# W_out's sums spread over all pairs with two sets of buffers; loads pinned behind operand loads; operands split three steps ahead

## The chip, the cores and the metric

The kernel runs on one core of one Trainium2 chip. The metric is the time of one execution on the device in microseconds, the median of several runs. The core has five engines that run their own instruction streams in order: TensorE (PE, matmuls), VectorE (DVE), ScalarE (ACT), GpSimd (POOL) and SyncE (SP, which here only issues DMAs). The program is written with tiles; a scheduler orders each engine's instructions by their place in the program and by when they are ready, and inserts the waits.

## The reference

One layer of an encoder on a sequence of 1024 tokens of width 1024, in float32. All three sub-layers stand between norms:

```
x = x + 1/2 * post1(SwiGLU_1(pre1(x)))      # feed-forward, D_FF = 2816
x = x + post_mix(token_mixing(pre_mix(x)))   # retention and neighbourhood attention
x = x + 1/2 * post2(SwiGLU_2(pre2(x)))      # feed-forward, D_FF = 2816

def _swiglu(x, w_in, w_out):
    g, u = jnp.split(x @ w_in, 2, axis=-1)
    return (jax.nn.silu(g) * u) @ w_out

def _rms_norm(x, gain):
    y = x * lax.rsqrt(jnp.mean(x * x, axis=-1, keepdims=True) + RMS_EPS)
    return y * gain
```

The change touches the two feed-forward sub-layers only.

## The kernel before, in words

Every float32 operand is split into a high and a low part (`Core.split`, lines 60 and 61: a cast on ACT, then a subtraction on DVE), and each product is three matmuls (`mm3`, lines 87 to 89: high x high, low x high, high x low). A matmul here has 128 x 128 weights and 512 columns. The large products use the Winograd form of Strassen's scheme: seven half-sized products and a number of sums in place of eight products.

A feed-forward has two stages.

`ffn_in` computes silu(x Wg) * (x Wu), transposed, in 22 *pairs* (a gate block and an up block of 128 features, index i). In one pair `Pairs.run` does seven products of twelve matmuls (P1, P6, P2, P7, P5, P4, P3 in this order); DVE makes the weight-side sums in place in the raw weights (`wraw`), splits them (`wh`, `wl`, eight buffers each), and adds the results up. `done(j)` is called as a quarter of the result is ready, in the order 0, 3, 1, 2; with j = 1 and 2 it multiplies gate and up into the tile `gt` (line 416). After every second pair `LeftFactors` makes four sums of two `gt` tiles on POOL (tile `cmb`, line 440) and stores seven blocks to DRAM (`g0a`, `g0s`; in the second feed-forward `g1a`, `g1s`) with DMAs that POOL issues (line 67). These are the left operands of the next stage.

In passing, `ffn_in` also prepares the weight-side sums of `W_out` for the next stage: `OutSums` takes eleven sets of four 128 x 512 blocks of `W_out`, loads them (line 521, SP), makes four subtractions on DVE (line 524) and stores the four results to DRAM (POOL, tensor `t`). Before the change it is a generator that does one step (four loads, or one subtraction with its store) at each call of `done`, four in a pair, from pair 6 on in the first feed-forward and from pair 4 on in the second. Its tiles are `lead` in the pool `early` in the first (six buffers, shared with what the lead products save), `tw` in the second (four buffers). Nothing fixes where in its engine's order a step comes; the scheduler may move it forward.

`ffn_out` computes the down-projection in seven products (a11, s1, s2, s3, a22, a12, s4) of eleven *steps* each, 77 in all. A step takes one left block (`Blocks`: load `graw` on SP, split into `gh`, `gl`) and one weight block (`wraw`, split into `wh`, `wl`), and does twelve matmuls, three into each of four banks. `operand(n)` prepares step n; before the change, steps n and n + 1 are prepared ahead of the matmuls of step n. There are four buffers for `gh` and `gl`: three in the pool `gl10` and one in `gl11` in the first feed-forward, two in `gl20` and two in `gl21` in the second. After the eleventh step of a product, its handler (p1, p5, p6, p7, p4, p2, p3) takes the four banks out on ACT or DVE; `more` in p7 queues two further sums and a square for each of four token tiles, which are taken up one per step from product a22 on. `Epilogue` holds the norm: gains (loaded in step 11), squares on ACT (line 481) with a product with the gain (line 482, POOL unless told otherwise), and the residual. The rows of x for it come by `xload` in the steps 30 to 36 and 57 to 63 of the program.

Memory: pools lie in stacks from the left and the right. In the first feed-forward the left stack holds, from the same base, first `norm1`, then `fin1` (`c0` and `c1` with two 2 KB buffers each, `gt` with three of 4 KB: 20 KB per partition), then the pools of `ffn_out`: 20 KB (`mid0`), then `gl10` with 18 KB. In the second, `cmb2` (8 KB) and `tw2` (8 KB) lie below `fin2` (20 KB), and the pools of `ffn_out` begin with 36 KB (`out2`), then `gl21` with 12 KB; `gl20` is on the right. A tile of a new pool may be written as soon as the old tiles under it are released.

Of the kernel before, what the change touches and what calls it, by code (L numbers as in the profile page):

```python
# [10 lines left out]
F32 = mybir.dt.float32  # L11
F32R = mybir.dt.float32r
AF = mybir.ActivationFunctionType
ALU = mybir.AluOpType
# [4 lines left out]
P = 128  # L19
# [5 lines left out]
FT = DFF // P  # L25
# [12 lines left out]
class Core:  # L38
# [131 lines left out]
class Filler:  # L170
# [13 lines left out]
    def __call__(self, n):  # L184
        for _ in range(n):
            if not self.step():
                return
# [216 lines left out]
def ffn_in(c, pairs, pool, put, sums):  # L404

    nc = c.nc
    for i in range(FT):
        gate = [pool.tile([P, 512], F32, tag=f"c{j}", name=f"c{j}", bufs=2) for j in range(2)]
        gt = pool.tile([P, S], F32, tag="gt", name="gt", bufs=3)
        up = gt[:, :512], gt[:, 512:]  # L410

        def done(j):
            if j < 2:
                nc.scalar.activation(gate[j], gate[j], AF.Silu)  # L414
            if j in (1, 2):
                nc.vector.tensor_tensor(up[j % 2], gate[j % 2], up[j % 2], ALU.mult)
            sums(i)
        pairs.run(i, (*gate, *up).__getitem__, done)
        put(i, gt)

# [24 lines left out]
class Blocks:  # L445
# [6 lines left out]
    def __call__(self, src):  # L452
        p = self.pools[self.n % len(self.pools)]
        self.n += 1
        r = p.tile([P, 512], F32, tag="graw", name="graw", bufs=self.raws[p is not self.pools[0]])
        self.c.nc.sync.dma_start(r, src)
        a = [p.tile([P, 512], F32R, tag=g, name=g, bufs=self.pools.count(p)) for g in ("gh", "gl")]
        self.c.split(*a, r)
        return a
# [47 lines left out]
class OutSums:  # L507


    def __init__(self, c, tile, src, dst, first):  # L510
        self.first, self.left = first, self.steps(c, tile, src, dst)

    @staticmethod
    def steps(c, tile, src, dst):

        tt = c.nc.vector.tensor_tensor
        for k in range(FT // 2):
            ks = slice(k * 512, (k + 1) * 512)
            b11, b12, b21, b22 = b = [tile() for _ in range(4)]
            for q in range(4):  # L520
                c.nc.sync.dma_start(b[q], src[q][:, ks])
            yield
            for n, o, x, y in ((0, b11, b12, b11), (2, b12, b22, b12), (1, b22, b22, b11), (3, b21, b21, b22)):
                tt(o, x, y, ALU.subtract)
                c.store(dst[n][:, ks], o)
                yield

    def __call__(self, i):
        if i >= self.first:
            next(self.left, None)  # L530


def ffn_out(c, q, blocks, junk, xtile, w_out, t_out, gl, ep, side={}):


    nc = c.nc
    NK = FT // 2
    tt, add = nc.vector.tensor_tensor, nc.gpsimd.tensor_tensor
    later, rest, flips, xs = [], [], [], {}

    def xload(t):

        xs[t] = xtile(t)
        nc.sync.dma_start(xs[t], ep.resid(t))


    def p1(u, b):
        nc.scalar.copy(q[0][:, u], b)

    def p6(u, b):  # L550
        tt(q[1][:, u], b, q[0][:, u], ALU.add)

    def p5(u, b):
        nc.scalar.copy(q[2][:, u], b)

    def p7(u, b):
        tt(q[3][:, u], b, q[1][:, u], ALU.add)

        def more():
            add(q[1][:, u], q[1][:, u], q[2][:, u], ALU.add)  # L560
            add(q[2][:, u], q[3][:, u], q[2][:, u], ALU.add)
            ep.square(u, 1, q[2][:, u], junk[u])
        later.extend((more, None))

    def p4(u, b):
        tt(q[3][:, u], b, q[3][:, u], ALU.add)
        ep.square(u, 0, q[3][:, u], b)
        later.extend(stages(u, (q[3][:, u], q[2][:, u])))

    def stages(t, halves):  # L570
        g = ep.steps(t, xs[t], halves)

        f = []
        return [lambda: next(g), lambda: next(g)] + [
            lambda: f.append(next(g)), lambda: f[0](*(("ps", 6) if i < 6 else ("pt", 2)))] * (ep.pre is not None)

    def p2(u, b):
        tt(q[0][:, u], b, q[0][:, u], ALU.add)
        ep.square(4 + u, 0, q[0][:, u], b)

    def p3(u, b):
        e = tt(q[1][:, u], b, q[1][:, u], ALU.add)
        out = q[1][:, u] if ep.pre is not None else q[3][:, u]
        ep.square(4 + u, 1, q[1][:, u], b if ep.pre is not None else junk[2 + u % 2], out, nc.vector if u == 3 else nc.gpsimd)
        g = ep.steps(4 + u, xs[4 + u], (q[0][:, u], out))
# [12 lines left out]
    steps = [(i, k) for i in range(len(products)) for k in range(NK)]  # L598
    xloads = {n: j for j, n in enumerate((30, 32, 34, 36, 57, 59, 61, 63))}
    operands, raws, banks, last = {}, {}, {}, []  # L600

    def wraw(n):

        if n not in raws:
            raw = c.wpool.tile([P, D], F32, tag="wraw", name="wraw", bufs=3)
            (i, k), two = steps[n], n + 1 < len(steps) and steps[n][1] < NK - 1
            nc.sync.dma_start(raw[:, :512 + 512 * two], products[i][1][:, k * 512:(k + 1 + two) * 512])
            raws[n] = raw[:, :512]
            if n + 1 < len(steps):
                if not two:  # L610
                    nc.sync.dma_start(raw[:, 512:], products[i + 1][1][:, :512])
                raws[n + 1] = raw[:, 512:]
        return raws.pop(n)

    def operand(n):
        if n < len(steps) and n not in operands:
            i, k = steps[n]
            operands[n] = blocks(gl[products[i][0]][:, k * 512:(k + 1) * 512]), c.piece(wraw(n))

    def one(u, k, a, b):  # L620
        c.mm3(banks[u], [p[:, u * P:(u + 1) * P] for p in a], b, k == 0, k == NK - 1)

    for n, (i, k) in enumerate(steps):
        for m in range(2):
            operand(n + m)
        if n == NK:
            ep.gains()
        if n in side:
            side[n]()
        if n in xloads:  # L630
            xload(xloads[n])
        if later and i > 3:
            f = later.pop(0)
            if f:
                f()
        if k == 0:
            banks = {u: c.bank() if i % 2 == 0 or u < 2 else c.bank("pt", 2) for u in range(4)}
        ab = operands.pop(n)
        if i == len(products) - 1 and k >= NK - 4:
            last.append((k, *ab))  # L640
        else:
            for u in range(4):
                one(u, k, *ab)
        if k == NK - 1:
            operand(n + 2)
            for u in range(4):
                for e in last:
                    one(u, *e)
                products[i][2](u, banks[u])
    assert not later  # L650
    return flips
# [354 lines left out]
def trunk_layer(ctx: ExitStack, tc, x, g1a, w1i, w1o, g1b, gma, wmt, wnv, wrv, logits, dtab, rope, bias,  # L1006
                wro, wno, wmo, gmb, g2a, w2i, w2o, g2b, out):
    nc = tc.nc
# [36 lines left out]
    with tc.tile_pool(name="norm1", bufs=1, reuse_waits="tile") as ep:  # L1045
# [7 lines left out]
                f()  # L1053
        fin = Pairs(c, wx, [(w1i[i], w1i[FT + i]) for i in LeftFactors.order], 3, 3)
        fin.lead(lambda: early.tile([P, 512], F32, tag="lead", name="lead", bufs=6), on_pool=(3, 4, 5, 0))
    with tc.tile_pool(name="fin1", bufs=1, reuse_waits="tile") as fp:
        ffn_in(c, fin, fp, LeftFactors(c, early, gl[0]),
               OutSums(c, lambda: early.tile([P, 512], F32, tag="lead", name="lead", bufs=6), w1o, t1o, 6))
    right.close()

    x0pool = pool(right, "x0", "right")
# [4 lines left out]
    ep = pool(ep_stack, "ep1", "right")  # L1066
# [244 lines left out]
    tw = pool(left, "tw2")  # L1311
    with tc.tile_pool(name="fin2", bufs=1, reuse_waits="tile") as fp:
        ffn_in(c, fin, fp, LeftFactors(c, cmb, gl[1]),
               OutSums(c, lambda: tw.tile([P, 512], F32, tag="tw", name="tw", bufs=4), w2o, t2o, 4))
    left.close()
    a_stack.close()
    g_stack.close()
# [89 lines left out]
```

## Time and profile before

| | us |
|---|---|
| median of 3 runs (lowest, highest) | 2358.86 (2357.84, 2363.87) |
| the profiled execution | 2363.65 |
| its span, first to last instruction | 2361.9 |
| PE busy | 2240.7 |
| DVE busy | 1704.5 |
| ACT busy | 1001.7 |
| POOL busy | 626.7 |

The first `ffn_in` runs from about 60 us to 486 us of the span, its `ffn_out` to about 740; the token mixing follows; the second `ffn_in` runs from about 1707 to 2137 us, and its `ffn_out` to the end. A row of stretches gives the busy time of each engine and, behind x, the number of its instructions in that stretch. A row of waits names the waiting engine with its line, what released it, the sum, the number and the longest. A row of the timeline gives start and duration in us and, in brackets, how long the engine was idle before and what ended it. A row of a tile gives the shortest, median and longest duration in ns, and the first and last start in us. PE instructions overlap, so PE counts as busy at a low clock too; the number of matmuls in a stretch tells more.

### The profile page before, as it was taken

To read this page: it belongs to the slowest core of one execution; us is meant where nothing else is said; L and a number is where in the kernel's file an instruction comes from. 1 tells how busy PE (TensorE), PEld (TensorE's weight loads), DVE (VectorE), ACT (ScalarE), POOL (GpSimd) and SP (SyncE) were. 2 spreads that over 40 slices of the span, in tenths; PEclk is the share of its full clock that TensorE was granted. 3 is DMA by queue.
4 is the path that set the end of the run, shared out by engine and by line. 5 is a ranking of instruction groups with operands and counts; after the bars stand their busy time and mean duration, and the time that the engine had idled before them with its cause. 6 is when DMAs were issued, how large, how long until landed. Compare 5 with 4: busy or idle time off the path is not lost.

```text
span 2361.9 us, 30397 instructions
## 1 busy us (share of the span) xinstructions
PE 2240.7 (95%) x10288; PEld 1846.2 (78%) x10288; DVE 1704.5 (72%) x2921; ACT 1001.7 (42%) x2102; POOL 626.7 (27%) x713
## 2 busy tenths in 40 slices
PE   6998899989998999999999999999799999999998
PEld 5776688868777787787888888887577778888876
DVE  7887686645588758879985678547898787665566
ACT  6332232334455323248885675226533232234443
POOL 5243331310224123411101222101533323221042
PEclk9999999989999999999999999999899999999999
DMA  4357632376564443247755467856466543337655
GB/s 143 132 191 240 231 130 95 122 254 190 175 200 139 164 161 112 103 160 241 232 178 170 156 221 236 292 208 207 155 218 211 199 148 123 104 122 272 192 161 172
DMA packets 163677, 422.64 MB, mean 179 GB/s; under 512 B 19713, under 2 KB 47489, under 8 KB 163457
## 3 DMA queue, kind: packets, MB, share of 16 engines
q1 hardware_dynamic: 130080, 310.04, 41.2%
q0 software_dynamic: 33440, 110.65, 11.9%
q8 instruction: 81, 1.33, 0.2%
q14 instruction: 76, 0.61, 0.1%
HBM read 301.60 MB, written 123.21 MB: 180 GB/s over the span
## 4 chain that ended last, share of the span: by engine, by line
PE 63%; DVE 13%; issue 8%; POOL 8%; DMA 6%; ACT 2%; SPq 0%; POOLq 0%; DVEq 0%; ACTq 0%
PE ps L89 19%; PE ps L87 19%; PE ps L88 19%; DVE wl L61 2%; POOL cmb L440 2%; PE pt L87 1%; PE pt L88 1%; PE pt L89 1%; POOL rstd L97 1%; PE ps L721 1%; PE pt L740 1%; DMA t<-tw 1%; POOL t L67 1%; DMA graw<-g0a 1%; DMA t<-lead 1%
## 5 line engine op out<-in xcount | busy, mean ns | idle before, releaser
L61 DVE TENSOR_TENSOR wl<-wraw,wh 128x512 fp32r<-128x512 f32 x662 | 491.9, 764 | 81.3 <-ACT wh L60 80.2
L60 ACT CAST wh<-wraw 128x512 fp32r<-128x512 f32 x670 | 391.1, 617 | 244.5 <-PE ps L88 84.3
L61 DVE TENSOR_TENSOR gl<-graw,gh 128x512 fp32r<-128x512 f32 (+2 forms) x178 | 130.9, 736 | 188.8 <-ACT gh L60 188.6
L87 PE MATMUL ps<-wh,gh 128*128 128x512 f32 x612 | 241.9, 397 | 15.7 <-ACT gh L60 14.6
L89 PE MATMUL ps<-wh,gl 128*128 128x512 f32 x612 | 241.3, 397 | 4.2 <-DVE gl L61 3.9
L88 PE MATMUL ps<-wl,gh 128*128 128x512 f32 x612 | 241.2, 395 | 2.0 <-DVE wl L61 2.0
L60 ACT CAST gh<-graw 128x512 fp32r<-128x512 f32 (+2 forms) x178 | 107.0, 601 | 234.5 <-PE ps L88 100.2
L414 ACT ACTIVATE c<-c 128x512 f32<-128x512 f32 x88 | 55.6, 632 | 296.9 <-DVE c L384 199.1
L87 PEld LDWEIGHTS ps<-wh,gh 128*128 128x128 f32 x612 | 116.7, 191 | 43.1 <-ACT gh L60 17.3
L89 PEld LDWEIGHTS ps<-wh,gl 128*128 128x128 f32 x612 | 116.6, 191 | 33.2 <-DVE gl L61 8.9
L88 PEld LDWEIGHTS ps<-wl,gh 128*128 128x128 f32 x612 | 116.8, 191 | 26.8 <-DVE wl L61 3.1
L60 ACT CAST wh<-t 128x512 fp32r<-128x512 f32 x58 | 36.1, 622 | 220.2 <-DVE t L378 218.8
L89 PE MATMUL ps<-s2h,wl 128*128 128x512 f32 x232 | 97.5, 420 | 21.4 <-DVE wl L61 21.4
L89 PE MATMUL ps<-a12h,wl 128*128 128x512 f32 x280 | 110.6, 395 | 3.7 <-DVE wl L61 3.7
L87 PE MATMUL ps<-a11h,wh 128*128 128x512 f32 x280 | 111.9, 400 | 1.4 <-ACT wh L60 0.7
L87 PE MATMUL ps<-a12h,wh 128*128 128x512 f32 x280 | 111.5, 398 | 0.0
L89 PE MATMUL ps<-a11h,wl 128*128 128x512 f32 x280 | 110.5, 395 | 0.7 <-DVE wl L61 0.7
L88 PE MATMUL ps<-a11l,wh 128*128 128x512 f32 x280 | 110.8, 396 | 0.0
L88 PE MATMUL ps<-a12l,wh 128*128 128x512 f32 x280 | 110.0, 393 | 0.0
L87 PE MATMUL ps<-a22h,wh 128*128 128x512 f32 x280 | 109.8, 392 | 0.0
L89 PE MATMUL ps<-a22h,wl 128*128 128x512 f32 x280 | 109.1, 390 | 0.0
L88 PE MATMUL ps<-a22l,wh 128*128 128x512 f32 x280 | 109.0, 389 | 0.0
(356 smaller groups left out, 5969.8 us busy)
## 6 DMA issues: line engine op xcount, KB each, us to landing
wraw<-in_dram SPq DMA_DIRECT2D x243, 512.0 KB, 4.4
wraw<-t SPq DMA_DIRECT2D x40, 512.0 KB, 3.7
lead<-in_dram SPq DMA_DIRECT2D x44, 256.0 KB, 4.0
g0s<-cmb POOLq DMA_DIRECT2D x44, 256.0 KB, 2.5
t<-lead POOLq DMA_DIRECT2D x44, 256.0 KB, 3.5
graw<-g0s SPq DMA_DIRECT2D x44, 256.0 KB, 2.8
tw<-in_dram SPq DMA_DIRECT2D x44, 256.0 KB, 3.4
t<-tw POOLq DMA_DIRECT2D x44, 256.0 KB, 3.7
```

The costliest lines, as they stand in the source:

```text
L60: nc.scalar.copy(h, src)
L61: (eng or nc.vector).tensor_tensor(l, src, hf, ALU.subtract)
L67: self.nc.gpsimd.dma_start(dst, src)
L87: mm(ps, a[0], b[0], start=start, stop=False)
L88: mm(ps, a[0], b[1], start=False, stop=False)
L89: mm(ps, a[1], b[0], start=False, stop=stop)
L97: self.nc.gpsimd.tensor_tensor(r[:, :n], ms, self.mhalf[:, :n], ALU.pow)
L414: nc.scalar.activation(gate[j], gate[j], AF.Silu)
L440: eng.tensor_tensor(s[o], a, b, op)
L721: nc.tensor.matmul(bv, q[:, rg * P:(rg + 1) * P], k, start=n == 0, stop=n == 1)
L740: nc.tensor.transpose(pt[:, j * P:(j + 1) * P], s[:, i % 2, (i // 2) * P:(i // 2 + 1) * P], c.ident)
```

## The change

`OutSums` is rewritten. Set 0 is loaded in pair 0, set k in pair 2k - 1; set 0 is subtracted in pair 1, two subtractions each at `done(1)` and `done(2)`; set k in pairs 2k and 2k + 1, one at each of these. The call is made inside `issue_after(e.ins)`, which puts what the call makes on the engine of `e` (DVE) behind `e`, the product that has just written `gt`; it is an order in that engine's queue, not a wait. The loads (SP) and stores (POOL) are on other engines. There are eight buffers (two sets) in both feed-forwards; in the first they are a pool of their own, `tw1`, opened below `fin1`.

In `ffn_out` the loads of x and of the gains are put behind the last operand load on SP, the operands of steps n, n + 1 and n + 2 are prepared ahead of the matmuls of step n (and n + 3 ahead of a product's handler), and the sums and the gain product of `more` go from POOL to DVE.

```diff
@@ ffn_in
             if j in (1, 2):
-                nc.vector.tensor_tensor(up[j % 2], gate[j % 2], up[j % 2], ALU.mult)
-            sums(i)
+                e = nc.vector.tensor_tensor(up[j % 2], gate[j % 2], up[j % 2], ALU.mult)
+                with c.tc.issue_after(e.ins):
+                    sums(i, j)
@@ Blocks
-        self.c.nc.sync.dma_start(r, src)
+        self.load = self.c.nc.sync.dma_start(r, src)
@@ OutSums
-        for k in range(FT // 2):
...
-            for n, o, x, y in ((0, b11, b12, b11), (2, b12, b22, b12), (1, b22, b22, b11), (3, b21, b21, b22)):
-                tt(o, x, y, ALU.subtract)
-                c.store(dst[n][:, ks], o)
-                yield
-    def __call__(self, i):
-        if i >= self.first:
-            next(self.left, None)
+    def load(self, k):
+        self.b[k] = [self.tile() for _ in range(4)]
+        for t, src in zip(self.b[k], self.src):
+            self.c.nc.sync.dma_start(t, src[:, k * 512:(k + 1) * 512])
+    def sub(self, k, n):
+        b11, b12, b21, b22 = self.b[k]
+        o, x, y = ((b11, b12, b11), (b22, b22, b11), (b12, b22, b12), (b21, b21, b22))[n]
+        self.c.nc.vector.tensor_tensor(o, x, y, ALU.subtract)
+        self.c.store(self.dst[n][:, k * 512:(k + 1) * 512], o)
+    def __call__(self, i, j):
+        if j == 1 and (i == 0 or i % 2 == 1 and i < FT - 2):
+            self.load((i + 1) // 2)
+        for n in ((0, 2), (1, 3))[j - 1] if i == 1 else ():
+            self.sub(0, n)
+        if i > 1:
+            self.sub(i // 2, (0, 2, 1, 3)[i % 2 * 2 + j - 1])
@@ ffn_out
         xs[t] = xtile(t)
-        nc.sync.dma_start(xs[t], ep.resid(t))
+        with c.tc.issue_after(blocks.load.ins):
+            nc.sync.dma_start(xs[t], ep.resid(t))
...
-            add(q[1][:, u], q[1][:, u], q[2][:, u], ALU.add)
-            add(q[2][:, u], q[3][:, u], q[2][:, u], ALU.add)
-            ep.square(u, 1, q[2][:, u], junk[u])
+            tt(q[1][:, u], q[1][:, u], q[2][:, u], ALU.add)
+            tt(q[2][:, u], q[3][:, u], q[2][:, u], ALU.add)
+            ep.square(u, 1, q[2][:, u], junk[u], eng=nc.vector)
...
-        for m in range(2):
+        for m in range(3):
             operand(n + m)
         if n == NK:
-            ep.gains()
+            with c.tc.issue_after(blocks.load.ins):
+                ep.gains()
...
-            operand(n + 2)
+            operand(n + 3)
@@ trunk_layer
+    with (tc.tile_pool(name="tw1", bufs=1, reuse_waits="tile") as tw,
+          tc.tile_pool(name="fin1", bufs=1, reuse_waits="tile") as fp):
-               OutSums(c, lambda: early.tile([P, 512], F32, tag="lead", name="lead", bufs=6), w1o, t1o, 6))
+               OutSums(c, lambda: tw.tile([P, 512], F32, tag="tw", name="tw", bufs=8), w1o, t1o))
...
-               OutSums(c, lambda: tw.tile([P, 512], F32, tag="tw", name="tw", bufs=4), w2o, t2o, 4))
+               OutSums(c, lambda: tw.tile([P, 512], F32, tag="tw", name="tw", bufs=8), w2o, t2o))
```

More of the change, by code (lines that the diff above doesn't have):

```diff
@@ L507, with __init__ @@
 class OutSums:
[L510 to L516, printed above, removed]
-        for k in range(FT // 2):
[L518 to L521, printed above, removed]
-            yield
-            for n, o, x, y in ((0, b11, b12, b11), (2, b12, b22, b12), (1, b22, b22, b11), (3, b21, b21, b22)):
-                tt(o, x, y, ALU.subtract)
-                c.store(dst[n][:, ks], o)
-                yield
-    def __call__(self, i):
-        if i >= self.first:
-            next(self.left, None)
+    def __init__(self, c, tile, src, dst):
+        self.c, self.tile, self.src, self.dst, self.b = c, tile, src, dst, {}
+    def load(self, k):
[14 more added lines that the diff above has]
+            self.sub(i // 2, (0, 2, 1, 3)[i % 2 * 2 + j - 1])
 def ffn_out(c, q, blocks, junk, xtile, w_out, t_out, gl, ep, side={}):
@@ L537, in ffn_out @@
     NK = FT // 2
-    tt, add = nc.vector.tensor_tensor, nc.gpsimd.tensor_tensor
+    tt = nc.vector.tensor_tensor
     later, rest, flips, xs = [], [], [], {}
@@ L1055, in trunk_layer @@
         fin.lead(lambda: early.tile([P, 512], F32, tag="lead", name="lead", bufs=6), on_pool=(3, 4, 5, 0))
-    with tc.tile_pool(name="fin1", bufs=1, reuse_waits="tile") as fp:
+    with (tc.tile_pool(name="tw1", bufs=1, reuse_waits="tile") as tw,
+          tc.tile_pool(name="fin1", bufs=1, reuse_waits="tile") as fp):
         ffn_in(c, fin, fp, LeftFactors(c, early, gl[0]),
-               OutSums(c, lambda: early.tile([P, 512], F32, tag="lead", name="lead", bufs=6), w1o, t1o, 6))
+               OutSums(c, lambda: tw.tile([P, 512], F32, tag="tw", name="tw", bufs=8), w1o, t1o))
     right.close()
```

## The prediction

> **What bounds the kernel now.** I read the page's busy times first, then stretches of the span, then who waited for whom inside the bad stretches, then the timeline of single gaps.
>
> ```profile
> span 2361.9 us, 30397 instructions
> ```
> ```profile
> PE 2240.7 (95%) x10288; PEld 1846.2 (78%) x10288; DVE 1704.5 (72%) x2921; ACT 1001.7 (42%) x2102; POOL 626.7 (27%) x713
> ```
>
> TensorE is the bound, and its 95% hides how much it misses: at a low clock its instructions last longer and still count as busy. So I count matmuls in stretches that lie where the change acts (columns: start:end, length, then busy us and count for PE, weight loads, DVE, ACT, POOL, then granted clock, DMA share, GB/s).
>
> ```profile
> 130.00:310.00 180.00, 161.13 (x666) 129.73 (x665) 139.03 (x211) 45.79 (x81) 74.84 (x91) 0.94 0.64 223
> 310.00:480.00 170.00, 170.00 (x752) 140.76 (x751) 120.09 (x183) 53.70 (x94) 42.95 (x51) 1.00 0.33 116
> 480.00:511.00 31.00, 20.89 (x81) 16.66 (x80) 13.63 (x17) 7.45 (x13) 8.71 (x10) 0.78 0.74 257
> 511.00:620.00 109.00, 109.00 (x482) 90.26 (x481) 55.53 (x87) 49.41 (x88) 1.29 (x1) 1.00 0.66 209
> 620.00:640.00 20.00, 16.75 (x66) 12.63 (x65) 12.62 (x12) 8.58 (x19) 16.04 (x11) 0.93 0.26 70
> 1712.00:1732.00 20.00, 17.44 (x71) 14.03 (x70) 19.35 (x27) 8.78 (x14) 7.09 (x7) 0.91 0.45 158
> 1732.00:1930.00 198.00, 184.69 (x781) 148.46 (x780) 161.36 (x239) 54.24 (x98) 73.55 (x95) 0.97 0.61 207
> 1930.00:2130.00 200.00, 200.00 (x884) 165.62 (x883) 138.48 (x214) 62.70 (x110) 48.57 (x56) 1.00 0.32 113
> 2130.00:2250.00 120.00, 120.00 (x531) 99.34 (x531) 64.31 (x96) 53.18 (x95) 8.71 (x10) 1.00 0.71 236
> 2258.00:2278.00 20.00, 16.79 (x66) 12.63 (x65) 12.60 (x12) 8.58 (x19) 16.01 (x11) 0.94 0.26 73
> ```
>
> The row from 310 shows TensorE undisturbed: 752 matmuls in 170 us, 0.226 us each. That is the second half of the first up-projection (`ffn_in`), after the old `OutSums` had ended; 1930 to 2130 is the same place in the second. Against 0.226 us the other rows are short:
> - A, 130 to 310, `ffn_in` with the sums of `W_out`: 796 fit, 666 ran, 130 x 0.226 = 29.4 us lost.
> - B, 1732 to 1930, the same in the second: 876 against 781, 21.5 us.
> - C, 480 to 511, where the first `ffn_out` begins: 137 against 81, 12.7 us.
> - D, 620 to 640 and 2258 to 2278, after product `s3` of each `ffn_out`: 88.5 against 66, 5.1 us each.
> - E, 1712 to 1732, the start of the second `ffn_in`: 88.5 against 71, 4.0 us.
> - 2130 to 2250, where the second `ffn_out` begins: 531 of 531, nothing lost.
>
> In all 77.8 us are on the table. Now the causes of A and B: VectorE's waits in 130 to 310, SyncE's queue there, and VectorE's in 1730 to 1930.
>
> ```profile
> DVE lead L524 <- DMA lead<-in_dram: 35.1, 7, 7.9
> ```
> ```profile
> SPq L521 <- DMA t<-lead: 74.0, 30, 11.2
> ```
> ```profile
> DVE tw L524 <- DMA tw<-in_dram: 21.4, 9, 6.2
> DVE gl L61 <- ACT gh L60: 9.2, 2, 6.0
> ```
>
> VectorE works in order, and it stands for 35.1 and 21.4 us behind a subtraction whose block hasn't landed. The block is late because its load waits on SyncE for the store of the previous block from the same buffer: six buffers for sets of four in the first stage, four in the second. One gap, on SP, DVE and PE:
>
> ```profile
> 207.29 23.19 SPq L521 DMA_DIRECT2D lead<-in_dram  x6
> ```
> ```profile
> 222.83 0.69 DVE L524 TENSOR_TENSOR lead<-lead 128x512 f32<-128x512 f32 x1 [7.90 <-DMA lead<-in_dram]
> ```
> ```profile
> 225.38 0.79 PE L89 MATMUL ps<-s2h,wl 128*128 128x512 f32 x1 [6.56 <-DVE wl L61]
> 225.97 0.63 PE L87 MATMUL ps<-s2h,wh 128*128 128x512 f32 x1
> 226.39 0.63 PE L88 MATMUL ps<-s2l,wh 128*128 128x512 f32 x1
> ```
>
> SP spends 23 us over six loads, DVE waits 7.90 us, the split of P6's weights is late, PE stands 6.56 us and then starts matmuls every 0.42 us instead of 0.226: each gap is paid a second time in clock.
>
> **The change, part by part.**
>
> *Sums of W_out.* As many instructions as before: 44 loads, 44 subtractions, 44 stores per stage. Now set k is loaded in pair 2k-1 and subtracted in pairs 2k and 2k+1, two per pair, over all 22 pairs. A set of buffers comes round again only after its stores have had a whole pair (19 us) to land, and a load has a pair to land; the longest waits shown are 7.9 and 11.2 us. So the waits of A and B should go. What it costs where there were no sums (310 to 480): two subtractions a pair on DVE.
>
> ```profile
> L524 DVE TENSOR_TENSOR lead<-lead x44: 674/692/1798, 120.4 to 303.2; 128x512 f32<-128x512 f32 x44
> ```
>
> 2 x 0.692 = 1.4 us a pair; DVE was busy 120.09 of 170 us there, so idle 49.9 us, or 5.6 us in each of nine 19 us pairs. The pin puts a subtraction behind the `up` product; behind it queue the splits for the next pair, which PE wants. The cover is that 5.6 us; without it 22 pairs x 1.4 = 31 us a stage would show. Lower bound of what stays in A: 0, as in 310 to 480; upper bound 9, one gap like the one shown with its slow start. I take 3 for A (eight loads now come in the first two pairs) and 4 for B, where some early splits stay (below). Gains 26.4 and 17.5. In E two subtractions fewer stand before the sum that PE waits for: 1.0 us.
>
> *Where the new buffers lie.* Eight 2 KB buffers are a 16 KB pool below `fin1`, which moves up from 0 to 16 KB (second stage: from 16 to 24 KB). The pools of `ffn_out` do not move. In the first stage, the three operand buffers `gl10` (20 to 38 KB) lay above `fin1` (0 to 20 KB) and were free early, so three operands were split in the middle of `ffn_in`; now `fin1` (16 to 36 KB) covers them until its last `gt` tile is released. Rows: the casts from 60 to 500 us; the loads of x; the gap on PE; the last POOL sum that reads `gt`.
>
> ```profile
> L60 ACT CAST gh<-graw x6: 618/622/625, 91.1 to 494.7; 128x512 fp32r<-128x512 f32 x6
> ```
> ```profile
> L544 SPq DMA_DIRECT2D xs<-in_dram x8: 333/430/1499, 491.0 to 516.5; - x8
> ```
> ```profile
> 494.45 0.39 PE L89 MATMUL ps<-wh,gl 128*128 128x512 f32 x1
> 504.95 0.79 PE L87 MATMUL ps<-wh,gh 128*128 128x512 f32 x1 [10.11 <-ACT gh L60]
> ```
> ```profile
> 494.06 1.29 POOL L440 TENSOR_TENSOR cmb<-gt,cmb 128x512 f32<-128x512 f32 x1
> ```
>
> Before: PE ran the three early operands (36 matmuls, 8.1 us, to 494.5) and then waited 10.11 us for the fourth, whose load had company: the loads of x, 512 KB each, begin at 491.0. After: the first operand can be cast only once POOL has read the last `gt`, 494.06 + 1.29 = 495.4, and is on PE at 496.0, where PE is free at 486.5 (36 x 0.226 before 494.6). The gap is 9.5 us, and with the 2.6 that C lost beside its gap (12.7 - 10.1) C becomes 12.1, a gain of 0.6. Bounds: 0 if the first three stay early after all and the fourth's load, without company, is in time; 18 if the fourth is late as well.
>
> In the second stage, the second and fourth operands (`gl21`, 36 to 48 KB) come under `gt` (32 to 44 KB); the first and third, in a pool on the other side, stay early. Rows: PE's first matmul of `ffn_out`, POOL's two sums that free the `gt` of pair 20, and PE's gap at the start of that stage.
>
> ```profile
> 2137.55 0.39 PE L87 MATMUL ps<-wh,gh 128*128 128x512 f32 x1
> ```
> ```profile
> 2139.72 3.01 POOL L440 TENSOR_TENSOR cmb<-gt 128x512 f32<-128x512 f32 x2 [1.78 <-DVE gt L416]
> ```
> ```profile
> 1722.90 0.76 PE L87 MATMUL ps<-s1h,wh 128*128 128x512 f32 x1 [2.56 <-DVE gt L381]
> 1723.46 0.63 PE L88 MATMUL ps<-s1l,wh 128*128 128x512 f32 x1
> 1723.88 0.63 PE L89 MATMUL ps<-s1h,wl 128*128 128x512 f32 x1
> ```
>
> PE runs out at 2137.55 + 12 x 0.226 = 2140.3; the second operand is cast (0.62) after 2142.73, so at 2143.4: a new gap F of 3.1 us. After the 2.56 us gap PE started matmuls 0.42 us apart, so I add 1.4 us (seven of them 0.2 late): 4.5 us lost where nothing was. Bounds 0 and 8. [...]
>
> *Sums of product s3 onto DVE.* Per `ffn_out`, eight additions and four gain products leave POOL. POOL's groups from 610 to 640, one split of DVE, one square of ACT:
>
> ```profile
> L561 POOL TENSOR_TENSOR q<-q 128x512 f32<-128x512 f32 x4 | 6.0, 1510 | 0.1
> L560 POOL TENSOR_TENSOR q<-q 128x512 f32<-128x512 f32 x4 | 6.0, 1514 | 121.8 <-DVE q L557 121.8
> L482 POOL TENSOR_TENSOR q<-q,gain 128x512 f32<-128x512 f32 x4 | 5.6, 1400 | 0.8 <-ACT junk L481 0.8
> ```
> ```profile
> 631.90 1.77 DVE L61 TENSOR_TENSOR wl<-wraw,wh 128x512 fp32r<-128x512 f32 x1
> ```
> ```profile
> 626.48 0.64 ACT L481 ACTIVATE junk<-q 128x512 f32<-128x512 f32 x1 [3.86 <-POOL q L561]
> ```
>
> 17.6 us on POOL become 12 x 0.692 = 8.3 us on DVE. While POOL sums, a split takes 1.77 instead of 0.69 us, and ACT, in order, holds the next casts behind a square that waits 3.86 us for POOL. Both go. Cover for the 8.3 us: DVE is busy 55.53 of 109 us in 511 to 620, so 10.7 us idle in the eight steps of 2.7 us over which the code spreads these sums. I leave 0.5 of each D: gain 9.2 (bounds 0, if the squares wait for DVE as long, and 10.2).
>
> *Pinned loads of x and gains, operands three ahead.* Eight loads of x and two of gains leave the start of `ffn_out` and go behind operand loads on SP; what queues behind them are operand loads that wait for a free buffer anyway. Needed only 18 or more steps (49 us) later. Row: the casts' waits, whole span.
>
> ```profile
> ACT gh L60 <- PE ps L88: 100.2, 60, 5.2
> ```
>
> Casts already wait for PE to give a buffer back, so they run as far ahead as four buffers allow; an earlier place in the program changes nothing in the steps. At the end of a product the evictions now stand behind one more cast and split, and the next product uses other banks. I take 0, bounds -2 and +2 (a loss if an eviction is late, a gain if the start of C gets less crowded).
>
> *Sum:* 26.4 + 17.5 + 1.0 + 0.6 - 4.5 + 9.2 = 50.2 us. The profiled execution took 2363.65 us, 1.75 more than its span, and 4.8 more than the median 2358.86: 2313 on its own footing, 2309 against the median, which I give.
>
> **Rivals.**
> 1. *The loads wander.* The pin binds only what runs on DVE; loads of a set stay free on SP. Placed as soon as a set's stores are expected, they hold SP as in the 74.0 us of waits, and weights come late instead of blocks. Against it: a pair of slack. It keeps half of A and B: 22 us less, 2331.
> 2. *Stretched subtractions reach PE.* The pin sets one subtraction in each odd pair right where POOL begins its four sums of `gt`. The next rows show the splits after that `up` product with POOL at work (pair ending at 412) and without (431).
>
> ```profile
> 412.38 2.39 DVE L61 TENSOR_TENSOR wl<-wraw,wh 128x512 fp32r<-128x512 f32 x2
> ```
> ```profile
> 431.42 1.29 DVE L61 TENSOR_TENSOR wl<-wraw,wh 128x512 fp32r<-128x512 f32 x2
> ```
>
> So 1.1 us more in each of 22 odd pairs, 24 us if nothing hides it: 2333. Against it: PE lost nothing there in 310 to 480. [...]
> 3. *C goes.* If `gl10` isn't covered, the first three operands stay early, and if the fourth's load then has no company, nothing of C is left: 12 us better, 2297. Against it: the sizes of the pools as the code gives them.
> 4. *Slower.* A set's load stands on SP behind a load of weights that waits for its buffer until the pair's end, and every set comes late: 40 sets (20 a stage after the first) at 7.9 us and some 2 of clock, less the cover. It decides from 50.2 / 40 = 1.3 us a set; at a third of the shown price, 3.3 us, it gives 2309 + 132 = 2441. Against it: a load has 19 us, and a load with free buffers is ready before one without.
>
> **How the numbers follow.** Forecast 0.60, rival 1 0.15, rival 2 0.09, rival 3 0.08, rival 4 0.05, nothing measurable (the pins give an order that was there already, and new gaps eat the rest) 0.03. The likeliest gives 2309. Rivals 1 to 3 span 2297 to 2333; the bounds of C, F and D (6 below to 12 above) widen this to 2294 to 2337. Faster by over 0.3% (7 us, about what a measurement of this kernel can tell from no change) 0.92, same 0.03, slower 0.05.
>
> **What would show it.** After the change: no wait of a `tw` subtraction for its load above 1 us; 750 or so matmuls in any 170 us of `ffn_in`; no operand cast in the first `ffn_in`; a PE gap near 9.5 us where the first `ffn_out` begins and near 3 us in the second's second operand; additions of L560 and L561 on DVE at 0.7 us, splits there at 0.7, no gap after `s3`. I am wrong if DVE waits for `tw` loads or weights in every pair, or if the starts of `ffn_out` lose over 20 us.

## The result: 53 us less, and the profile after

The changed kernel takes 2305.16 us (2303.96 to 2306.69), the kernel before 2358.35 us (2357.57 to 2363.87) in the same comparison: a ratio of 0.977, 95% interval 0.9753 to 0.9787. The forecast was 2309. The profiled execution of the changed kernel took 2306.69 us. First its page's span and busy times:

```profile
span 2304.8 us, 30361 instructions
PE 2218.8 (96%) x10288; PEld 1839.6 (80%) x10288; DVE 1675.8 (73%) x2945; ACT 1003.4 (44%) x2102; POOL 593.1 (26%) x689
```

The span is 57.1 us shorter than the profiled one of before. Then the stretches that answer to A to F (start:end, length, busy us and count for PE, weight loads, DVE, ACT, POOL, then granted clock, DMA share, GB/s):

```profile
92.00:270.00 178.00, 177.84 (x785) 146.95 (x784) 148.84 (x230) 56.57 (x99) 64.22 (x80) 1.00 0.53 179
270.00:450.00 180.00, 180.00 (x795) 149.02 (x794) 127.87 (x206) 54.36 (x95) 60.07 (x73) 1.00 0.49 163
450.00:475.00 25.00, 15.13 (x57) 11.95 (x56) 11.45 (x18) 7.19 (x12) 9.58 (x12) 0.80 0.61 211
580.00:604.00 24.00, 24.00 (x107) 19.88 (x106) 20.49 (x34) 12.73 (x26) 0.00 (x0) 1.00 0.62 187
1676.00:1696.00 20.00, 19.47 (x87) 15.80 (x86) 18.90 (x27) 8.37 (x15) 5.48 (x4) 1.00 0.22 74
1696.00:1880.00 184.00, 184.00 (x813) 152.39 (x812) 144.23 (x228) 57.22 (x102) 63.07 (x77) 1.00 0.53 178
1880.00:2072.00 192.00, 192.00 (x848) 158.97 (x847) 138.82 (x224) 59.90 (x105) 62.77 (x75) 1.00 0.47 158
2072.00:2092.00 20.00, 12.86 (x45) 10.02 (x44) 9.99 (x15) 5.03 (x9) 10.04 (x12) 0.75 0.67 223
2200.00:2240.00 40.00, 40.00 (x178) 33.15 (x177) 29.11 (x48) 21.95 (x46) 3.97 (x4) 1.00 0.65 205
```

The pitch of an undisturbed stretch is 192 / 848 = 0.2264 us. By it, what each place loses (length / 0.2264, less the matmuls that ran, times 0.2264):

| place | before | forecast | after | from the row |
|---|---|---|---|---|
| A, first `ffn_in` | 29.4 | 3 | 0.3 | 92: 786.2 fit, 785 ran |
| B, second `ffn_in` | 21.5 | 4 | 0 | 1696 and 1880: all ran |
| C, first `ffn_out` starts | 12.7 | 12.1 | 12.1 | 450: 110.4 fit, 57 ran |
| D, after `s3`, two places | 10.2 | 1 | 0 | 580 and 2200: all ran |
| E, second `ffn_in` starts | 4.0 | 3 | 0.3 | 1676: 88.3 fit, 87 ran |
| F, second `ffn_out` starts | 0 | 4.5 | 9.8 | 2072: 88.3 fit, 45 ran |

The table gives 77.8 - 22.5 = 55.3 us; the spans differ by 57.1, the medians by 53.2.

VectorE's waits in the first `ffn_in` (60 to 480) no longer hold a wait for a block of `W_out`; the two largest are on PE's results. SyncE's queue in the same stretch waits for the stores more than before (104.0 us against 74.0), and nobody pays for it:

```profile
DVE c L389 <- PE ps L89: 34.5, 18, 2.0
DVE c L384 <- PE ps L89: 27.4, 16, 1.9
```
```profile
SPq L517 <- DMA t<-tw: 104.0, 28, 6.5
```

The subtractions themselves, and how they lie in 40 slices of the span (shortest, median and longest ns; first and last start in us):

```profile
L522 DVE TENSOR_TENSOR tw<-tw x88: 677/683/1186, 96.6 to 2078.1; 128x512 f32<-128x512 f32 x88
...
busy tenths in 40 slices 0111111100000000000000000000011111110000
```

C is the first gap below, with the cast that ends it and the wait of SyncE just ahead (timelines of PE and ACT, waits of SyncE). The cast starts when the store of a `gt` block has landed; POOL's last sum over `gt` ended 0.7 us before it, at 464.75:

```profile
466.16 0.80 PE L87 MATMUL ps<-wh,gh 128*128 128x512 f32 x1 [9.87 <-ACT gh L60]
```
```profile
465.49 0.62 ACT L60 CAST gh<-graw 128x512 fp32r<-128x512 f32 x1 [8.72 <-DMA g0a<-gt]
```
```profile
SPq L457 <- DMA g0a<-gt: 6.5, 1, 6.5
```

F, in the second stage, on PE, ACT, POOL and SyncE:

```profile
2086.12 0.79 PE L87 MATMUL ps<-wh,gh 128*128 128x512 f32 x1 [7.14 <-ACT gh L60]
```
```profile
2085.45 1.25 ACT L60 CAST gh<-graw 128x512 fp32r<-128x512 f32 x2 [5.52 <-DMA graw<-g1a]
```
```profile
2078.28 3.31 POOL L441 TENSOR_TENSOR cmb<-gt 128x512 f32<-128x512 f32 x2 [1.18 <-DVE gt L416]
```
```profile
SPq L457 <- POOL cmb L441: 0.7, 1, 0.7
```

POOL's two sums end at 2081.59. I had let the cast follow them directly; but a load, too, waited on SyncE for that sum, and the cast at 2085.45 for a load to land.

### The profile page after: what moved, and what is told of

Same layout as the page of the kernel before. It is cut to its first block, busy times and chain, and to the rows that moved or that the text cites. A ratio compares the mean times of both kernels' runs of the same rounds, so it can differ in the third digit from the quotient of the medians.

```text
span 2304.8 us, 30361 instructions
## 1 busy us (share of the span) xinstructions
PE 2218.8 (96%) x10288; PEld 1839.6 (80%) x10288; DVE 1675.8 (73%) x2945; ACT 1003.4 (44%) x2102; POOL 593.1 (26%) x689
## 4 chain that ended last, share of the span: by engine, by line
PE 80%; DVE 11%; issue 3%; POOL 3%; DMA 1%; ACT 1%; SPq 0%; POOLq 0%; DVEq 0%; ACTq 0%
PE ps L89 25%; PE ps L87 24%; PE ps L88 24%; DVE wl L61 2%; PE pt L89 1%; PE pt L87 1%; PE pt L88 1%; POOL rstd L97 1%; PE ps L725 1%; PE pt L744 1%; POOL cmb L287 1%; DVE tmp L117 1%; DVE t L378 1%; POOL cmb L288 1%; DVE xs L493 1%
## 5 line engine op out<-in xcount | busy, mean ns | idle before, releaser
L61 DVE TENSOR_TENSOR wl<-wraw,wh 128x512 fp32r<-128x512 f32 x662 | 468.9, 728 | 80.4 <-ACT wh L60 79.4
L61 DVE TENSOR_TENSOR gl<-graw,gh 128x512 fp32r<-128x512 f32 (+2 forms) x178 | 124.3, 699 | 173.8 <-ACT gh L60 173.6
L483 POOL TENSOR_TENSOR q<-q,gain 128x512 f32<-128x512 f32 x22 | 33.6, 1546 | 357.7 <-ACT ps L482 343.4
L89 PE MATMUL ps<-a12h,wl 128*128 128x512 f32 x280 | 110.4, 394 | 3.7 <-DVE wl L61 3.7
```

The costliest lines, as they stand in the source:

```text
L61: (eng or nc.vector).tensor_tensor(l, src, hf, ALU.subtract)
L89: mm(ps, a[1], b[0], start=False, stop=stop)
L483: (eng or c.nc.gpsimd).tensor_tensor(h if out is None else out, h, self.post[:, b * 512:(b + 1) * 512], ALU.mult)
```

## Experiments

The ratios are against the kernel before, run beside each.

**1. The sums of `s3` alone.** In the kernel before, only the additions of `more` and the gain product go to DVE.

```
-            add(q[1][:, u], q[1][:, u], q[2][:, u], ALU.add)
-            add(q[2][:, u], q[3][:, u], q[2][:, u], ALU.add)
-            ep.square(u, 1, q[2][:, u], junk[u])
+            tt(q[1][:, u], q[1][:, u], q[2][:, u], ALU.add)
+            tt(q[2][:, u], q[3][:, u], q[2][:, u], ALU.add)
+            ep.square(u, 1, q[2][:, u], junk[u], eng=nc.vector)
```

> The kernel before, with only the eight additions and four gain products of p7 moved from POOL to DVE in each ffn_out. Theory (POOL's sums stretch DVE's splits and hold ACT's casts behind its squares): the gaps D go, 5.6 and 5.8 us by the trace of before, so 11 us less, 2347. Rival (the squares just wait for DVE instead of POOL, and DVE's 8.3 us more work delays the splits): under 4 us less, 2354 or more.

2351.32 us, ratio 0.9964 (0.995 to 0.9978). Its stretches around `s3`:

```profile
610.00:640.00 30.00, 30.00 (x134) 24.88 (x133) 23.52 (x39) 15.13 (x30) 0.00 (x0) 1.00 0.63 198
2250.00:2280.00 30.00, 30.00 (x134) 24.88 (x133) 22.51 (x37) 17.48 (x39) 2.84 (x2) 1.00 0.59 185
```

30 / 0.2264 = 132.5: all matmuls ran, D is gone in both places. The 8 us of the medians are somewhat less than the 10.2 of the two gaps.

**2. The sums of `W_out` alone.** The changed kernel with the parts in `ffn_out` undone.

```
-        with c.tc.issue_after(blocks.load.ins):
-            nc.sync.dma_start(xs[t], ep.resid(t))
+        nc.sync.dma_start(xs[t], ep.resid(t))
... (gains likewise; two steps ahead; sums of s3 on POOL)
```

> The changed kernel without its parts in ffn_out: only the sums of W_out spread, with two sets of buffers and their pin; loads of x and gains unpinned, operands two ahead, p7's sums on POOL. Theory: A, B and E go (about 55 us), the new gap F of 10 us stays, D stays with 11 us: 2305 + 11 = 2316; without the pins on the loads C may cost up to 8 us more, 2324. Rival (part of A and B went by the pinned loads or by the lookahead): 2330 or more.

2324.25 us, ratio 0.9854 (0.9838 to 0.9871). The first `ffn_in` is as in the changed kernel. In its profile D is back (10.9 us in the two places), and C and F are larger: PE waits 13.38 and 9.56 us there, against 9.87 and 7.14. These 16.8 us are most of the 19 by which the medians differ.

**3. Without the pin on the sums.**

```
-                with c.tc.issue_after(e.ins):
-                    sums(i, j)
+                sums(i, j)
```

> The changed kernel without issue_after around the call of the sums; all else as changed. Theory (the spread alone took A and B away; the pin only names a place): within 4 us of the changed kernel, 2301 to 2309. Rival (without the pin the scheduler moves subtractions forward to where their loads should just have landed, and DVE stands for loads again): DVE waits for tw loads of 10 us or more in each ffn_in, 2320 or more.

2337.54 us, ratio 0.9905 (0.9887 to 0.9923): 32 us of the gain go. The program still spreads the sums over 22 pairs, but look at where they ran:

```profile
L521 DVE TENSOR_TENSOR tw<-tw x88: 673/684/1923, 62.9 to 1830.5; 128x512 f32<-128x512 f32 x88
...
busy tenths in 40 slices 0432000000000000000000000000045100000000
```

The scheduler drew them all forward to the start of each `ffn_in`: the 44 of the first stage start between 62.9 and 195.3 us, over six in the time of a pair. (That it goes by an estimate of when a load is done is my reading; no row shows it.) DVE and PE in the second stage show one price:

```profile
1781.44 2.01 DVE L521 TENSOR_TENSOR tw<-tw 128x512 f32<-128x512 f32 x3
...
1789.37 0.69 DVE L521 TENSOR_TENSOR tw<-tw 128x512 f32<-128x512 f32 x1 [4.30 <-DMA tw<-in_dram]
```
```profile
1794.81 0.79 PE L87 MATMUL ps<-s2h,wh 128*128 128x512 f32 x1 [5.17 <-ACT wh L60]
```

Subtractions in a row, then one in front of DVE's queue whose block has not landed, behind it the weight sums of P6, then PE. This is A's chain again, with two full sets of buffers. It explains most of what the second stage loses; DVE waits 12.8 us for blocks there. The first stage pays in another way. DVE waits little for blocks there, but from 92 to 160 us it is busy with hardly a pause, and the sums and splits that PE wants queue behind subtractions that are ready. At 141.18, for instance, two of them take 3.72 us ahead of the sums of P6, and PE then waits until 148.07 (waits of DVE from 60 to 480, two stretches, DVE):

```profile
DVE tw L521 <- DMA tw<-in_dram: 4.7, 3, 3.5
```
```profile
92.00:130.00 38.00, 35.15 (x145) 27.71 (x144) 35.40 (x56) 10.74 (x18) 15.84 (x23) 0.96 0.79 272
130.00:160.00 30.00, 28.00 (x116) 22.37 (x115) 30.00 (x44) 9.05 (x16) 13.02 (x18) 0.94 0.74 260
```
```profile
141.18 3.72 DVE L521 TENSOR_TENSOR tw<-tw 128x512 f32<-128x512 f32 x2
```

300.4 matmuls fit into these two stretches and 261 ran: 8.9 us lost, of which waits for a block explain little. So the pin does two things: it keeps a subtraction behind its load, and it keeps the subtractions from crowding.

**4. One set of buffers.** The changed kernel with four buffers in place of eight.

```
-  tw.tile([P, 512], F32, tag="tw", name="tw", bufs=8)
+  tw.tile([P, 512], F32, tag="tw", name="tw", bufs=4)
```

> The changed kernel with four tw buffers instead of eight in both stages: the same spread order and pins, but one set. Theory (the second set is what takes the wait for the stores away): the load of a set can start only when the last store of the set before has landed after the end of the odd pair, some 10 us, and DVE waits for it at the first subtraction in half of the pairs: 20 us or more lost, 2325 or more, even though tw2 is 8 KB again and F with its 10 us goes. Rival (two subtractions a pair instead of four are what did it; a set has 14 us from the end of its pair to the next subtraction): A and B stay away and F goes, 2295.

2293.09 us, ratio 0.9722 (0.9708 to 0.9737): faster than the change itself. Its stretches of the first `ffn_in` and of the start of the second `ffn_out`:

```profile
92.00:270.00 178.00, 177.85 (x785) 146.97 (x784) 148.74 (x230) 56.32 (x99) 64.28 (x80) 1.00 0.53 179
...
2060.00:2090.00 30.00, 30.00 (x134) 24.84 (x133) 20.69 (x28) 11.36 (x21) 10.15 (x12) 1.00 0.66 216
```

The same 785 matmuls as with two sets, so the second set carries nothing; and F is gone, as the smaller pool leaves `gl21` in another place. "Two sets" was the wrong reason.

**5. Two steps ahead**, the rest as changed.

```
-        for m in range(3):
+        for m in range(2):
...
-            operand(n + 3)
+            operand(n + 2)
```

> The changed kernel with operands two steps ahead as before (and operand(n + 2) at a product's end). Theory (four buffers set how far the splits run ahead): no difference, 2302 to 2308. Rival (the third step helped where ffn_out begins or at a product's end): 3 us or more slower, 2308 or more, with new gaps on PE inside ffn_out.

2305.62 us, ratio 0.9778 (0.9758 to 0.9799): no difference from the changed kernel.

**6. Loads of x and gains not pinned**, the rest as changed (the first edit of experiment 2, with the gains).

> The changed kernel without the pins on the loads of x and of the gains. Theory (ten loads of 512 KB at the start of ffn_out delay the first operand loads): the gap where ffn_out begins grows by 3 to 5 us in the first stage and by up to 3 in the second: 2308 to 2313. Rival (these loads are hidden, and the difference seen when only the sums were spread came from the lookahead): 2303 to 2307.

2312.29 us, ratio 0.9802 (0.9781 to 0.9822), 6.7 us above the kernel of experiment 5 that ran beside it. The two starts of `ffn_out` on SyncE and on PE:

```profile
458.60 1.06 SPq L546 DMA_DIRECT2D xs<-in_dram  x2
459.70 9.87 SPq L457 DMA_DIRECT2D graw<-g0a  x3
```
```profile
469.62 0.80 PE L87 MATMUL ps<-wh,gh 128*128 128x512 f32 x1 [13.22 <-ACT gh L60]
```
```profile
2091.54 0.79 PE L87 MATMUL ps<-wh,gh 128*128 128x512 f32 x1 [11.66 <-ACT gh L60]
```

Loads of x, 512 KB each, go out among the operand loads that PE is waiting for. The two gaps are 3.35 and 4.52 us longer than in the changed kernel, 7.9 in all by the profiles, somewhat more than the 6.7 of the medians.

**7. Two sets, in another place.** In the second stage the even and the odd sets get pools of their own above `fin2`, so that `gl21` lies over the odd sets and no longer over `gt`.

```
-    tw = pool(left, "tw2")
-    with tc.tile_pool(name="fin2", bufs=1, reuse_waits="tile") as fp:
+    with (tc.tile_pool(name="fin2", bufs=1, reuse_waits="tile") as fp,
+          tc.tile_pool(name="tw2e", bufs=1, reuse_waits="tile") as twe,
+          tc.tile_pool(name="tw2o", bufs=1, reuse_waits="tile") as two):
...
+  (twe, two)[k % 2].tile([P, 512], F32, tag="tw", name="tw", bufs=4)
```

> The changed kernel with both sets kept, but in the second feed-forward the pools lie otherwise: fin2 first, then four buffers for even sets, then four for odd ones, so that the operand buffers gl21 lie over the odd sets, which are done a pair before the end, and not over gt. Theory (F comes from gt of the last pairs lying over gl21): F goes, 10 us less, 2295, and A and B stay away. Rival (F comes from the number of loads or stores at the end of ffn_in): 2303 or more.

2295.16 us, ratio 0.9729 (0.9709 to 0.9749). Where its second `ffn_out` begins:

```profile
2050.00:2090.00 40.00, 40.00 (x178) 33.13 (x177) 31.13 (x44) 16.30 (x29) 11.78 (x15) 1.00 0.62 206
```

40 / 0.2264 = 176.7, and 178 ran: F is a matter of place alone.

**8. Eight buffers, the old generator.** The changed kernel with `OutSums` and its call as before (a step at each `done`, from pair 6 and pair 4, not pinned), with eight buffers in the new pools.

```
-                with c.tc.issue_after(e.ins):
-                    sums(i, j)
+            sums(i)
... (OutSums as before; bufs=8 in the new pools)
```

> The changed kernel with the old generator for the sums (a step at each call of done, from pair 6 and pair 4 on, no pin) and eight buffers in the new pools: two sets, not spread. Theory (two sets carry it): A and B mostly go, 5 us of each left: 2305 to 2318. Rival (the spread carries it: four steps a pair keep DVE and POOL's stores too dense): half of A and B stays, 2330.

2335.61 us, ratio 0.9902 (0.9888 to 0.9917). This looks like the price of packing the sums. But its subtractions lie where those of experiment 3 lay, though that program spreads them:

```profile
L524 DVE TENSOR_TENSOR tw<-tw x88: 675/686/1916, 62.9 to 1831.4; 128x512 f32<-128x512 f32 x88
```

Unpinned, the scheduler makes nearly the same of both programs, and the times agree within 2 us. So packing and the missing pin had to be told apart:

**9. Packed and pinned.** The changed kernel, pin and two sets kept, with four subtractions a pair in pairs 6 to 16.

```
... (the calls of the changed kernel are replaced by)
+        k = i - 6
+        if j == 1 and -1 <= k < FT // 2 - 1:
+            self.load(k + 1)
+        for n in ((0, 2), (1, 3))[j - 1] if 0 <= k < FT // 2 else ():
+            self.sub(k, n)
```

> The changed kernel with its pin and its two sets of buffers, but the sums packed as tightly as in the kernel before: set k is loaded in pair k + 5 and subtracted in pair k + 6, four subtractions a pair (two behind each product that writes gt), pairs 6 to 16, in both stages. Theory (the pin does it: it keeps the scheduler from drawing the sums forward into one another, and the density alone costs nothing): first ffn_in loses under 4 us against an undisturbed stretch, time 2303 to 2310. Rival (density costs as well: sets come round twice as fast, loads and stores have half the time, and DVE has two subtractions in a row ahead of splits that PE wants): waits of subtractions for their loads or gaps on PE return, 2315 to 2335.

2302.87 us, ratio 0.9767 (0.9753 to 0.978), as the changed kernel. Where the sums ran, and SyncE's wait for their stores between 60 and 480:

```profile
L522 DVE TENSOR_TENSOR tw<-tw x88: 682/689/696, 170.1 to 1979.5; 128x512 f32<-128x512 f32 x88
```
```profile
SPq L517 <- DMA t<-tw: 152.9, 27, 19.6
```

SyncE waits twice as long for stores as in the kernel before (152.9 against 74.0 us), and DVE not once for a block. Four subtractions a pair cost nothing behind the pin; the six and more of experiment 3 were not tried with it. A load held up on SyncE, 19.6 us at the longest, cost nothing here either: the subtraction that needs it stands late enough in DVE's queue.

**10. The pin alone, in the kernel before.** Packed sums as in 9, but with the next set loaded behind the last subtraction of a set, one set at a time, in the buffers and places of the kernel before; `ffn_out` as before.

```
... (the calls of the changed kernel are replaced by; k = i - 6)
+        for n in ((0, 2), (1, 3))[j - 1] if 0 <= k < FT // 2 else ():
+            self.sub(k, n)
+        if j == 2 and -1 <= k < FT // 2 - 1:
+            self.load(k + 1)
```

> The kernel before with one thing changed: the subtractions of W_out are pinned behind the products that write gt. The sums stay packed (four a pair, pairs 6 to 16), the buffers and their places are those of the kernel before (six shared ones in the first stage, four in the second), the next set is loaded right behind the last subtraction of a set, and ffn_out is as before. Theory (the pin alone carries A, B and E): A and B lose under 4 us each, C (12.7) and D (5.1 twice) stay, no gap at the second operand of the second ffn_out; 2359 less 50 is 2309 (2303 to 2315). Rival (with a single set the load comes right behind the stores it overwrites, and the pinned subtraction then stalls DVE in each pair): waits of tw subtractions for their loads, and 2320 or more.

2307.33 us, ratio 0.9779 (0.9762 to 0.9796). Its two `ffn_in`:

```profile
92.00:270.00 178.00, 175.55 (x771) 144.06 (x770) 150.03 (x229) 58.25 (x103) 61.74 (x76) 1.00 0.53 185
...
1680.00:1880.00 200.00, 197.75 (x871) 162.79 (x870) 161.88 (x251) 66.72 (x117) 68.36 (x80) 1.00 0.46 161
```

Lost: 786.2 - 771, or 3.4 us, and 883.4 - 871, or 2.8 us. The pin with its schedule, without more buffers and without spreading, gives as much as the whole change; the other parts of the change about cancel (D and the loads against F). The old generator itself, which does one step at each of the four `done` calls, was not run with a pin, so in the kernel before the pin is shown only together with this schedule.

**11. C: the first operands in another place.** One set of buffers as in 4, with `gl10` and `gl11` moved to the end of the stack in the first stage.

```
+    pool(mid, "gap").tile([P, 2048], F32, name="gap")
+    g0 = pool(mid, "gl10")
+    g1 = pool(mid, "gl11")
```

> The changed kernel with one set of buffers (2293 us) and, besides, the operand buffers of the first ffn_out (gl10, gl11) moved out from under the gt tiles, to a place that is free early. Theory (the 9 to 10 us gap where the first ffn_out begins, C, is a matter of place: the first operand cannot be cast before the stores of the last gt have landed): the first operands are cast inside ffn_in, C shrinks from 11 us lost to at most 2, and the time is about 2284 (2281 to 2287). Rival (the gap only moves to the fourth operand, as in the kernel before, where three were early and PE waited 10.1 us for the fourth): 2292 to 2294, with the gap 8 us later.

2295.1 us, ratio 0.9733 (0.9717 to 0.9749): no gain over experiment 4, and PE still waits 8.19 us at 464. The operands were not cast early: their first load went out at 453 only, and the run does not show why. What ends the gap is another thing than in the changed kernel. The cast that PE waits for needs a load that went out at 460.21, and by the profile SyncE held this load until DVE had split the operand loaded before it, a split that stood in DVE's queue behind the last products and subtractions of the stage (casts on ACT, splits on DVE, waits of SyncE):

```profile
463.51 0.62 ACT L60 CAST gh<-graw 128x512 fp32r<-128x512 f32 x1 [5.79 <-DMA graw<-g0a]
```
```profile
458.44 1.75 DVE L61 TENSOR_TENSOR gl<-graw,gh 128x512 fp32r<-128x512 f32 x1
```
```profile
SPq L457 <- DVE gl L61: 2.5, 1, 2.5
```

**12. C: the places of the kernel before.** The sums, buffers and places of experiment 10 with the rest of the change, so that three operands are cast early again and no load of x keeps the fourth company.

> The same packed, pinned sums in the buffers and places of the kernel before, with all the rest of the change (sums of s3 on DVE, loads of x and gains pinned, three steps ahead). Three operands of the first ffn_out are cast early again, and the loads of x no longer keep the fourth company. Theory A (the fourth operand then is in time: the 10.1 us gap of the kernel before was the company): C is gone, 2283 (2280 to 2288). Theory B (the fourth operand waits for the stores of the last gt blocks like the first one in the changed kernel, and early operands only move the gap 8 us later): C stays at 8 to 10, 2293 (2290 to 2297), as with one set in the new places.

2298.4 us, ratio 0.9744 (0.9724 to 0.9764). PE, and the cast that it waits for:

```profile
476.20 0.79 PE L87 MATMUL ps<-wh,gh 128*128 128x512 f32 x1 [9.25 <-ACT gh L60]
```
```profile
475.53 0.62 ACT L60 CAST gh<-graw 128x512 fp32r<-128x512 f32 x1 [7.63 <-DMA graw<-g0a]
```

With early operands and without company C stays, some 10 us later in the span. The profile's chain of work shows the load behind this cast, here and in the kernel before (start, us):

```profile
469.02 6.41 DMA graw<-g0a
```
```profile
496.92 7.26 DMA graw<-g0a
```

The load takes 6.41 us without the loads of x and 7.26 with them, where the median of these loads here is 2.8. The two gaps differ by as much. So the loads of x were about 1 of the 10.11 us; why this load is slow even without them no run shows.

## Why the prediction was right, and where it was not

The time was right, 2309 against 2305.16, in part by errors that cancel: 10.4 us more than forecast came from A, B, E and D, and 5.3 less from F. (The ends of the stated range, 2294 and 2337, do not follow from the bounds beside them: 6 below 2297 and 12 above 2333 are 2291 and 2345.)

- **A, B, E** went as forecast in kind (a subtraction no longer stands in DVE's queue ahead of its block) and more fully in size: 50.6 + 3.7 us gained against 43.9 + 1.0. I had left 3 and 4 us for gaps at the start that did not come. The extra subtractions where there had been none cost nothing, as their cover said.
- **The reason** for A and B was the step that failed. I wrote that a set comes round only after its stores have had a pair to land, so the buffers and the slack take the waits away. Experiment 4 takes the second set away and loses nothing; experiment 9 packs the sums, so that SyncE stands up to 19.6 us for one store, and loses nothing; experiment 10 does both and loses 3.4 and 2.8 us; experiment 3 takes the pin away and loses 32 us. My own rival 1 had the missing half: loads do stand on SP behind stores (104.0 us), but weights come in time and no subtraction waits. The stall was one of order in DVE's queue, and it is the pin that keeps the order: without it a subtraction stands ahead of its block (second stage of experiment 3) or ready subtractions crowd out the splits (first stage).
- **C** came out at 12.1 as forecast, by another releaser: the landing of the store of `gt` (9 us after PE's last matmul of the stage), not POOL's last read. The cast started only 0.7 us after that read, so that the number fits is partly luck. And the pinned loads belong in it: without the pins C's wait is 13.22 us. There is no one cause of C in all variants: in the changed kernel the store's landing ends it, in experiment 11 a load held up by DVE's queue, in experiment 12 and in the kernel before a slow operand load. Neither place nor company alone removed it, and what would is open.
- **F** is the mis-sized term: 9.8 us, not 4.5, above its upper bound of 8. I had put only the `gh` of the second operand under the `gt` of pair 20. A load into `graw` had to wait for POOL as well, so a DMA stood between POOL's sum and the cast: the wait was 7.14 us, not 3.1. The slow clock behind it (granted 0.50 from 2086 to 2092, matmuls 0.42 us apart) took the other 2.7, not 1.4. Experiments 4 and 7 remove it by place alone.
- **D** was right: 10.2 us gained, 9.2 forecast.
- **Pinned loads** I set at 0 within 2. Experiment 6 gives 6.7 us, in the length of C and F: in a start where PE waits for a 256 KB block, loads of 512 KB beside it count, and without the pins C and F would have come out longer than measured. Three steps ahead were 0, as forecast.
- **Rivals 2 to 4** did not happen: no loss in the odd pairs (813 and 848 matmuls at full pitch), C not gone, no set late.

The fastest kernel of these is the change with one set of buffers (experiment 4): 2293.09 us, 12 us below the change.

## What to carry to other kernels

When an in-order engine waits for a side task's DMA, first ask why the instruction stands at that place. Here the scheduler put it in front of work that was ready, and with eight buffers further forward than before (first subtraction at 62.9 us in experiment 8, at 120.4 in the kernel before, whose six buffers were also shared). Fix the place of the side task behind a late instruction of the main work, then try with the fewest buffers, since each extra pool moves what comes after it in memory. Where the first operands of a stage lie over the last tiles of the one before, follow the load buffer too, not only the tile that is computed.

## What the hardware showed

In these runs, whether a short wait of PE cost clock did not follow from its length. In experiment 3 PE waits 1.64 us, soon after it 0.36 us, and then starts matmuls 0.42 us apart, the pitch behind F's gap in the changed kernel, where the granted clock was 0.50; in experiment 10 it waits 2.25 us, more than both together, and, past some transpositions, starts them 0.23 us apart, the pitch of the rows with a granted clock of 1.00:

```profile
148.07 0.50 PE L87 MATMUL ps<-s2h,wh 128*128 128x512 f32 x1 [1.64 <-ACT wh L60]
...
149.17 0.53 PE L89 MATMUL ps<-s2h,wl 128*128 128x512 f32 x1 [0.36 <-DVE wl L61]
149.50 0.62 PE L87 MATMUL ps<-s2h,wh 128*128 128x512 f32 x1
149.92 0.63 PE L88 MATMUL ps<-s2l,wh 128*128 128x512 f32 x1
```
```profile
635.77 1.29 PE L126 MATMUL ps<-ident,q 128*128 128x128 f32 x8 [2.25 <-DVE q L504]
...
637.14 0.39 PE L88 MATMUL ps<-wl,gh 128*128 128x512 f32 x1
637.37 0.39 PE L89 MATMUL ps<-wh,gl 128*128 128x512 f32 x1
```

Of A I wrote that each gap is paid a second time in clock; experiment 10's was not. And the 1.4 us that I added to F's 3.1 was an estimate taken over from one gap, the 2.56 us one, that could be off either way: behind F's 7.14 us the clock took 2.7.
